# Norm factors spread over the partitions through a row in DRAM

## The chip, the cores and the metric

The kernel runs on one core of a Trainium2 chip. The metric is the time of one execution on the device in microseconds (us); a kernel's time is the median over its runs. Where the text names engines, PE is TensorE (PEld its weight loads), DVE is VectorE, ACT is ScalarE, POOL is GpSimd, and SP is SyncE, which here only issues DMAs. L700 means line 700 of the kernel before.

## The reference

One layer of a streaming encoder is computed for a prompt of 2048 tokens and a sample of 64 tokens, with 1024 features and 2816 hidden units in the MLP. All tensors are float32.

```
h  = rmsnorm(x, g1) * (1 + sc1) + sh1          # sc, sh, gt: six vectors made from the conditioning vector
u, q, k, v, o, gates = split(h @ w_in)
mix = concat(pool_mixer(u), mlstm(q, k, v, gates) normed per head, times sigmoid(o)) @ w_out
x  = x + gt1 * mix
h2 = rmsnorm(x, g2) * (1 + sc2) + sh2
a, g = split(causal depthwise conv of width 3 over (h2 @ w_up))
x  = x + gt2 * ((silu(g) * a) @ w_down)
y  = rmsnorm(x, g_final)
rmsnorm(x, g) = x * rsqrt(mean(x * x) + 1e-6) * g
```

Each of the three norms needs one factor per token, `rsqrt(mean(x * x) + 1e-6)`. It is this factor that the change is about.

## The kernel before

Activations lie transposed: features over the 128 partitions (8 tiles for 1024 features), tokens along the free axis. A factor per token has therefore to stand on all 128 partitions as the same row. The sums of squares over the partitions come out of matmuls (`rstd_rows`, `rstd_cols`, and in `final` a row of small matmuls), and POOL raises them to the power -0.5. They then stand as columns: token p of a chunk of 128 on partition p, one column to a chunk. Turning the columns into a row on all partitions is the work of two helpers.

`bcast` (attention stage) and `bcast_cols` (all later uses) do it in the same way. DVE multiplies the identity by the column, which gives diagonals. ACT rounds them to the matmul's float32r format, DVE takes the difference (the low half), and PE multiplies a matrix of ones by each half, so that every partition gets the sum over the diagonal, which is the row. ACT copies it from PSUM to a tile with the tag `rb`. Both are generators: each `yield` gives control back to the loop that feeds PE, and they are resumed by ticks between matmuls.

The work has two stages.

*Attention.* Four groups of 512 tokens, the last with the 64 sample tokens besides (576). For each group: the projections (`proj_v` at L1122, then per head `proj_qko`, then four projections for the pooling mixer in `U_ORDER`, all through `gemm` at L458), the mLSTM chunks, and the output projection `outproj`. Every product is three float32r matmuls (high times high, high times low, low times high), whose halves are made by ACT (L392) and DVE (L395) as the weights come in, some units ahead of PE. Side work stands in queues of generators: `bg[0]` to `bg[4]`, advanced by `tick(i)`, and `side`, advanced by `extra()`; `drain` runs a queue to its end. In queue 1 run `norm1` of the next group (squares, statistics, then `bcast`, whose result is in `box`), `norm_apply` of the next group (`modulate`, L559 to L562, which reads the row), and, during the last group, `norm_h` (L717), which applies the second norm to the first 704 tokens in 16 steps (8 tiles of features by two halves of 352 tokens) and stores the result in DRAM. The factors of the second norm are kept as columns in `RS2`, written at the end of each group by `rstd_rows` from `side`, or by `stat2` for the last group. In this stage a planner orders each engine's instructions; its estimates decide where a DMA stands in a queue.

*MLP.* Three groups of 704 tokens, `fgroups[0]` to `[2]`. Here the order on PE, ACT, DVE and POOL is that in which the program writes them; SP's is still the planner's. A `Pair` makes seven products (`product`, L1577, 12 matmuls of 352 columns each) in place of eight, from sums of operands that are made beforehand. ACT's copies from one PSUM bank to another (`seed`, L1624) stand between them. Each product ticks queue 0 twice and some places tick queue 1. The second half of the MLP follows in parts (L2143), or paired (`quad_down`, L2020). `prepare` (L791) runs in queue 1 and makes the operands of the next group: it spreads the factors of 704 tokens, loads the residual from DRAM (L801), norms it (L712, L715) and stores seven sums and their halves to DRAM (L813, issued from ACT). It runs for groups 1 and 2. `final` (L1878) runs in queue 0 during the next group's first part and applies the last norm to the group that has ended: statistics (L1884), `bcast_cols`, eight products on DVE (L1893) with four yields from one to the next, and a store for each (L1897). The residual's tiles are then loaded anew for the next group (L1865), once the store has read them, and the next sums into them are at L1992. The last group ends through another function, `final_end`.

Scratch tiles come from a ring of five in the attention stage (tag `scr`) and a ring of four in the MLP (tag `fscr`). Each `bcast` or `bcast_cols` takes three of them, for the diagonals and the two halves.

Of the kernel before, what the change touches and what calls it, by code (L numbers as in the profile page):

```python
# [9 lines left out]
F32 = mybir.dt.float32  # L10
F32R = mybir.dt.float32r
AF = mybir.ActivationFunctionType
ALU = mybir.AluOpType
# [51 lines left out]
def tile_layer(ctx: ExitStack, tc: tile.TileContext, xT, vecs, cst, rst, w_mod, w_ada, c_rows, w_qkou, w_v, w_pool,  # L65
# [21 lines left out]
    def m2_ps():  # L87
        return bank("m2")
# [11 lines left out]
    def scr():  # L100
        return sp.tile([P, TMAX], F32, tag="scr", name="scr")
# [427 lines left out]
    def bcast(rs, o, box):  # L529

        rb = sp.tile([P, TMAX], F32, tag="rb", name="rb", bufs=1)
        dg = scr()
        dh = sp.tile([P, TMAX], F32R, tag="scr", name="dh")
        dl = sp.tile([P, TMAX], F32R, tag="scr", name="dl")
        for (a, b, n, s) in o.tsegs:
            lo = a * P
            w = (b - a) * n
            v = dg[:n, lo:lo + w].rearrange("p (t c) -> p t c", c=n)
            dve.tensor_tensor(out=v, in0=ident[:n, :n].unsqueeze(1).broadcast_to([n, b - a, n]),
                              in1=rs[:n, a:b].unsqueeze(2).broadcast_to([n, b - a, n]), op=ALU.mult)  # L540
            act.activation(dh[:n, lo:lo + w], dg[:n, lo:lo + w], AF.Copy)
            dve.tensor_tensor(out=dl[:n, lo:lo + w], in0=dg[:n, lo:lo + w], in1=dh[:n, lo:lo + w].bitcast(F32),
                              op=ALU.subtract)
        yield
        yield
        for (a, b, n, s) in o.tsegs:
            lo = a * P
            w = (b - a) * n
            ps = m2_ps()
            pe.matmul(ps[:, :w], ones_r[:n, :], dh[:n, lo:lo + w], start=True, stop=False)  # L550
            pe.matmul(ps[:, :w], ones_r[:n, :], dl[:n, lo:lo + w], start=False, stop=True)
            act.activation(rb[:, lo:lo + w], ps[:, :w], AF.Copy)
        box.append(rb)
        yield

# [12 lines left out]
    RS2 = cp.tile([P, NCH], F32, tag="RS2", name="RS2")  # L568
    pool.memset(RS2, 0.0)
    RF = cp.tile([P, 6], F32, tag="RF", name="RF")  # L570
    pool.memset(RF, 0.0)

# [18 lines left out]
    def stat2(o, ssum):  # L591
        out = RS2[:, 4 * o.g:4 * o.g + len(o.chunks)]
        for _ in range(12):
            yield
        rstd_cols([ssum], o, out)
        yield

    def outproj(o, mix, between):
# [29 lines left out]
        if o.last:  # L628
            bg[0].append(stat2(o, ssum))
        else:  # L630
            side.append(rstd_rows(ssum, o, RS2[:, 4 * o.g:4 * o.g + len(o.chunks)], []))

# [40 lines left out]

    def bcast_cols(rs, t0, w, box, scr, r0=0):

        rb = scr("rb")
        dg, dh, dl = scr(), scr(F32R), scr(F32R)
        t = t0
        while t < t0 + w:
            c, a = divmod(t, P)  # L680
            n = 1
            if a == 0 and t + P <= t0 + w:
                n = (t0 + w - t) // P
                v = dg[:, t - t0:t - t0 + n * P].rearrange("p (t c) -> p t c", c=P)
                dve.tensor_tensor(out=v, in0=ident.unsqueeze(1).broadcast_to([P, n, P]),
                                  in1=rs[:, c:c + n].unsqueeze(2).broadcast_to([P, n, P]), op=ALU.mult)
                t += n * P
            else:
                e = min(P, a + t0 + w - t)
                dve.tensor_scalar(out=dg[:, t - t0:t - t0 + e - a], in0=ident[:, a:e], scalar1=rs[:, c:c + 1],  # L690
                                  scalar2=None, op0=ALU.mult)
                t += e - a
        yield
        act.activation(dh[:, :w], dg[:, :w], AF.Copy)
        dve.tensor_tensor(out=dl[:, :w], in0=dg[:, :w], in1=dh[:, :w].bitcast(F32), op=ALU.subtract)
        yield
        yield
        for lo in range(0, w, FH):
            ps = m2_ps()
            pe.matmul(ps[:, :FH], ones_r, dh[:, lo:lo + FH], start=True, stop=False)  # L700
            pe.matmul(ps[:, :FH], ones_r, dl[:, lo:lo + FH], start=False, stop=True)
            act.activation(rb[:, lo:lo + FH], ps[:, :FH], AF.Copy)
        box.append(rb)
        yield

    def normed(x, k, t0, w, rb, steps=(0, 1)):
# [10 lines left out]
    def norm_h(o, rows, scr):  # L717
# [11 lines left out]
        for h in range(2):  # L729
            yield from bcast_cols(RS2, o.t0 + h * FH, FH, box, lambda dt=F32: rows[10 + h] if dt == "rb" else scr(dt))  # L730
        for i, (t0, k) in enumerate(todo):
# [59 lines left out]
    def prepare(o, scr):  # L791

        box = []
        yield from bcast_cols(RS2, o.t0, FT, box, scr)
        yield
# [1082 lines left out]
    def final(o, x3, ssum):  # L1878
# [9 lines left out]
        box = []  # L1888
        yield from bcast_cols(RF, 0, FT, box, fscr)
        yield  # L1890
        yield
        for k in range(KD):
# [404 lines left out]
```

## Time and profile before

| | us |
|---|---|
| median of 3 runs | 2172.56 |
| lowest and highest run | 2170.78, 2175.88 |
| the profiled execution | 2170.94 |
| its span | 2169.1 |
| PE busy in the span | 2144.5 |
| DVE busy | 1629.4 |
| ACT busy | 1095.8 |
| POOL busy | 246.3 |

The span is what the profiler saw from the first to the last instruction; the execution's own time is 1.8 us longer. Busy times are not added up, since the engines work side by side. A row of a timeline gives start, duration, engine, line, operation, result and inputs, and how many instructions were merged, all in us from the start of the span. A row of a line's instructions gives the number, then the shortest, median and longest duration in ns, then the first and last start in us. A row of a stage gives its limits and width, then each engine's busy time with its number of instructions, then the granted PE clock (1 is full), the DMA engines' busy share and GB/s. A row of waits gives who waited for whom, the total in us, how often, and the longest. Rows of DMA issues end with the KB of each and the median time from issue to landing.

### The profile page before, as it was taken

How to read it: one execution, taken by the hardware profiler on the slowest of the kernel's cores; microseconds unless marked ns; L12 is line 12 of the kernel's file. 1: busy time of each engine (PE TensorE's matmuls, PEld its weight loads, DVE VectorE, ACT ScalarE, POOL GpSimd, SP SyncE). 2: the span in 40 equal slices, each digit the busy share in tenths (PEclk: the TensorE clock that was granted, in tenths of full speed). 3: DMA queues.
4: the chain of work that ended last, by engine and by line, in shares of the span. 5: the costliest groups of instructions: out<-in, count | busy, mean ns of one | idle time of the engine just before them, and what ended most of it. 6: DMA issues, size and time to landing. Idle time of an engine off the chain costs nothing.

```text
span 2169.1 us, 37944 instructions
## 1 busy us (share of the span) xinstructions
PE 2144.5 (99%) x13505; PEld 2041.6 (94%) x13505; DVE 1629.4 (75%) x3068; ACT 1095.8 (51%) x2182; POOL 246.3 (11%) x474
## 2 busy tenths in 40 slices
PE   8999999999999999999999999999999999999998
PEld 7788988888899999999999999999999999999998
DVE  5768769767964768797967668988886597887874
ACT  4455335334333446474636445655655365565554
POOL 0010001001000101010101220100100331111112
PEclk9999999999999999999999999999999999999999
DMA  8897988988886477888967976666668675555542
GB/s 313 305 325 254 348 327 278 344 324 289 279 310 221 155 250 236 290 291 303 346 216 247 322 257 210 233 218 203 224 222 278 221 255 182 175 176 187 175 160 78
DMA packets 245862, 543.63 MB, mean 251 GB/s; under 512 B 25252, under 2 KB 68772, under 8 KB 242856
## 3 DMA queue, kind: packets, MB, share of 16 engines
q1 hardware_dynamic: 236232, 518.89, 70.5%
q10 hardware_dynamic: 9440, 22.32, 2.6%
q8 instruction: 106, 1.74, 0.3%
q14 instruction: 84, 0.69, 0.1%
HBM read 415.12 MB, written 125.99 MB: 249 GB/s over the span
## 4 chain that ended last, share of the span: by engine, by line
PE 83%; DVE 5%; DMA 3%; issue 2%; ACT 1%; SPq 0%; POOL 0%; DVEq 0%; POOLq 0%; ACTq 0%
PE mm L1577 35%; PE mm L458 21%; PE mm L2143 12%; PE mm L2020 8%; PE mm L1122 3%; DVE wt L395 2%; PE m L1312 1%; PE m L1332 1%; PE m L1334 1%; PE m L1297 1%; DMA wt<-wsum 1%; DVE tg L1555 1%; DMA raw<-w_v 1%; DMA raw<-w_ada 0%; ACT tg L1550 0%
## 5 line engine op out<-in xcount | busy, mean ns | idle before, releaser
L1577 PE MATMUL mm<-hx,wt 128*128 128x352 f32 x5544 | 885.2, 321 | 0.8 <-DVE eg L1586 0.5
L1577 PEld LDWEIGHTS mm<-hx,wt 128*128 128x128 f32 x5544 | 878.9, 188 | 1.8 <-DVE wt L395 0.8
L458 PE MATMUL mm<-hl,wt 128*128 128x512 f32 (+2 forms) x1920 | 388.6, 357 | 0.0
L392 ACT ACTIVATE wt<-raw 128x512 fp32r<-128x512 f32 (+3 forms) x470 | 276.5, 597 | 180.6 <-PE mm L2143 49.7
L458 PEld LDWEIGHTS mm<-hl,wt 128*128 128x128 f32 x1920 | 316.3, 189 | 44.3 <-issue 1.1
L395 DVE TENSOR_TENSOR wt<-raw,wt 128x512 fp32r<-128x512 f32 (+3 forms) x470 | 312.7, 671 | 57.3 <-ACT wt L392 57.1
L2143 PE MATMUL mm<-av,wt 128*128 128x448 f32 (+1 forms) x1632 | 262.7, 322 | 0.0
L2143 PEld LDWEIGHTS mm<-av,wt 128*128 128x128 f32 x1632 | 250.4, 188 | 11.1
L1992 DVE SCALAR_TENSOR_TENSOR x<-mm,MOD,x 128x352 f32<-128x352 f32 (+3 forms) x360 | 167.5, 505 | 78.4 <-PE mm L2143 65.0
L2020 PE MATMUL mm<-av,wt 128*128 128x352 f32 x1344 | 220.8, 323 | 2.3 <-DVE x L1992 0.7
L2020 PEld LDWEIGHTS mm<-av,wt 128*128 128x128 f32 x1344 | 215.4, 188 | 5.4 <-DVE ea L1586 3.4
L1624 ACT ACTIVATE mm<-mm 128x352 f32<-128x352 f32 x196 | 87.8, 448 | 250.9 <-PE mm L1577 194.5
L458 PE MATMUL mm<-mx,wt 128*128 128x512 f32 (+1 forms) x960 | 183.1, 352 | 0.6 <-DVE scr L231 0.6
L458 PEld LDWEIGHTS mm<-mx,wt 128*128 128x128 f32 x960 | 159.4, 188 | 23.5 <-DVE scr L231 0.5
L1555 DVE SCALAR_TENSOR_TENSOR ta<-ea,V,ta 128x704 f32<-128x704 f32 (+1 forms) x132 | 125.7, 952 | 64.3 <-ACT ta L1550 51.9
L1555 DVE SCALAR_TENSOR_TENSOR tg<-eg,V,tg 128x704 f32<-128x704 f32 (+1 forms) x132 | 125.7, 953 | 59.9 <-ACT tg L1550 57.5
L395 DVE TENSOR_TENSOR wt<-wt 128x512 fp32r<-128x512 f32 x196 | 132.9, 684 | 12.8 <-ACT wt L392 12.7
L392 ACT ACTIVATE wt<-wt 128x512 fp32r<-128x512 f32 x196 | 120.1, 623 | 30.7 <-DMA wt<-wsum 25.4
L1764 ACT ACTIVATE tg<-tg 128x704 f32<-128x704 f32 (+1 forms) x66 | 52.4, 795 | 70.9 <-DVE tg L1555 70.9
L1533 POOL COPY ea<-UC 128x2 f32<-128x2 f32 x66 | 32.9, 498 | 483.4 <-DVE ta L1555 398.2
L1122 PE MATMUL mm<-wt,hl 128*128 128x256 f32 (+1 forms) x576 | 71.3, 284 | 0.0
L1122 PEld LDWEIGHTS mm<-wt,hl 128*128 128x128 f32 x576 | 70.4, 190 | 0.8 <-issue 0.6
(292 smaller groups left out, 2175.1 us busy)
## 6 DMA issues: line engine op xcount, KB each, us to landing
wt<-wsplit SPq DMA_DIRECT2D x132, 512.0 KB, 4.4
raw<-w_up SPq DMA_DIRECT2D x198, 256.0 KB, 4.1
wt<-hl_kept SPq DMA_DIRECT2D x96, 512.0 KB, 5.8
wt<-wsum SPq DMA_DIRECT2D x132, 256.0 KB, 5.0
wsplit<-wt SPq DMA_DIRECT2D x66, 512.0 KB, 5.8
w<-w_up SPq DMA_DIRECT2D x44, 512.0 KB, 5.8
wsum<-w SPq DMA_DIRECT2D x22, 1024.0 KB, 4.9
Bd<-fscr ACTq DMA_DIRECT2D x56, 352.0 KB, 4.3
```

What stands on the lines that cost most here:

```text
L392: act.activation(u.w[:, 0, :u.n], u.raw[:, :u.n], AF.Copy)
L395: dve.tensor_tensor(out=u.w[:, 1, :u.n], in0=u.raw[:, :u.n], in1=u.w[:, 0, :u.n].bitcast(F32), op=ALU.subtract)
L458: pe.matmul(ps[bi][:, :hi - lo], U[:, a, k % 4 * P:(k % 4 + 1) * P], mv[k][:, b, lo:hi], start=(at == 0 and pi == 0), stop=(k == order[-1] ...
L1122: pe.matmul(ps[ti][:n, :cols], h[4 * kh + k4][:, b, lo:lo + n], U[:, a, k4 % 2 * cols:(k4 % 2 + 1) * cols], start=(kh == 0 and k4 == 0 and ...
L1533: pool.tensor_copy(ext[:, 0:2], UC[:, f, :])
L1555: dve.scalar_tensor_tensor(out=t[:, :E], in0=ext[:, j:j + E], scalar=wc(j, f), in1=t[:, :E], op0=ALU.mult, op1=ALU.add)
L1577: pe.matmul(bk.t[:, :FH], U[:, a, kc * P:(kc + 1) * P], Bo.at(nm, kc, b), start=(first and kc == 0 and pi == 0), stop=(kc == 3 and pi == 2 ...
L1624: act.activation(to.t[:, :FH], bk.t[:, :FH], AF.Copy)
L1764: act.activation(self.tg[:, :E], self.tg[:, :E], AF.Silu)
L1992: dve.scalar_tensor_tensor(out=x3[n][:, a:b], in0=bk.t[:, a - lo:b - lo], scalar=gt2(n, s), in1=x3[n][:, a:b], op0=ALU.mult, op1=ALU.add)
L2020: pe.matmul(bk.t[:, :FH], U[:, a, c:c + P], quad.put(op, m, b), start=(first and m == 0 and pi == 0), stop=(m == 1 and pi == 2), skip_grou ...
L2143: pe.matmul(bks[i].t[:, :hi - lo], U[:, a, k % 4 * P:(k % 4 + 1) * P], av[k][:, b, lo:hi], start=(k == 0 and (a, b) == PASSES[0]), stop=(k ...
```

## The change

`bcast` and `bcast_cols` lose their diagonals, halves and matmuls. The columns are stored as a row of tokens in DRAM, and that row is loaded into the `rb` tile with a stride of zero over the partitions. All these DMAs are issued from ACT. `rows_out` stores and `spread_row` loads. For the second norm the row `r2d` is written when the statistics are made: `r2_out` stands behind `rstd_rows` in `side`, and `stat2` stores two yields after its statistics. `norm_h` then spreads both halves at once, followed by two yields in place of eight; `prepare` has two yields where it had five ahead of its first load. `final` stores the row four yields after its statistics in two DMAs (five whole chunks, and the rest of 64 tokens), spreads it five yields later, and its products begin five yields after that. The memsets of `RS2` and `RF` go. `final_end` and the first group's own norm stay as they were.

```diff
     def bcast(rs, o, box):
+        rd = dr.tile([TMAX], F32, tag=f"rn{o.g}", name=f"rn{o.g}")
+        rows_out(rd, rs, o)
+        yield
+        yield
         rb = sp.tile([P, TMAX], F32, tag="rb", name="rb", bufs=1)
-        dg = scr()
-        dh = sp.tile([P, TMAX], F32R, tag="scr", name="dh")
-        dl = sp.tile([P, TMAX], F32R, tag="scr", name="dl")
+        spread_row(rb, rd, 0, o.T)
+        box.append(rb)
+        yield
+
+    def rows_out(rd, rs, o):
         for (a, b, n, s) in o.tsegs:
             lo = a * P
...
+            act.dma_start(out=rd[lo:lo + (b - a) * n].rearrange("(c p) -> p c", p=n), in_=rs[:n, a:b])
+
+    def spread_row(out, rd, t0, w):
+        act.dma_start(out=out[:, :w], in_=rd[t0:t0 + w].unsqueeze(0).broadcast_to([P, w]))
...
     RS2 = cp.tile([P, NCH], F32, tag="RS2", name="RS2")
-    pool.memset(RS2, 0.0)
     RF = cp.tile([P, 6], F32, tag="RF", name="RF")
-    pool.memset(RF, 0.0)
+    r2d = dr.tile([NTOK], F32, tag="r2d", name="r2d")
...
         rstd_cols([ssum], o, out)
+        for _ in range(2):
+            yield
+        rows_out(r2d[o.t0:o.t0 + o.T], out, o)
+        yield
+
+    def r2_out(out, o):
+        rows_out(r2d[o.t0:o.t0 + o.T], out, o)
         yield
...
-            side.append(rstd_rows(ssum, o, RS2[:, 4 * o.g:4 * o.g + len(o.chunks)], []))
+            out = RS2[:, 4 * o.g:4 * o.g + len(o.chunks)]
+            side.append(rstd_rows(ssum, o, out, []))
+            side.append(r2_out(out, o))
...
-    def bcast_cols(rs, t0, w, box, scr, r0=0):
...
         for h in range(2):
-            yield from bcast_cols(RS2, o.t0 + h * FH, FH, box, lambda dt=F32: rows[10 + h] if dt == "rb" else scr(dt))
+            box.append(rows[10 + h])
+            spread_row(box[h], r2d, o.t0 + h * FH, FH)
+        yield
+        yield
...
     def prepare(o, scr):
         box = []
-        yield from bcast_cols(RS2, o.t0, FT, box, scr)
+        box.append(scr("rb"))
+        spread_row(box[0], r2d, o.t0, FT)
+        yield
         yield
...
         yield
         yield
         box = []
-        yield from bcast_cols(RF, 0, FT, box, fscr)
-        yield
-        yield
+        rd = dr.tile([6 * P], F32, tag=f"rf{o.g}", name=f"rf{o.g}")
+        for _ in range(2):
+            yield
+        nf, rest = divmod(FT, P)
+        act.dma_start(out=rd[:nf * P].rearrange("(c p) -> p c", p=P), in_=RF[:, :nf])
+        act.dma_start(out=rd[nf * P:FT].unsqueeze(1), in_=RF[:rest, nf:nf + 1])
+        for _ in range(5):
+            yield
+        box.append(fscr("rb"))
+        spread_row(box[0], rd, 0, FT)
+        for _ in range(5):
+            yield
```

More of the change, by code (lines that the diff above doesn't have):

```diff
@@ L529, in bcast @@
     def bcast(rs, o, box):
+        rd = dr.tile([TMAX], F32, tag=f"rn{o.g}", name=f"rn{o.g}")
+        rows_out(rd, rs, o)
+        yield
+        yield
         rb = sp.tile([P, TMAX], F32, tag="rb", name="rb", bufs=1)
-        dg = scr()
-        dh = sp.tile([P, TMAX], F32R, tag="scr", name="dh")
-        dl = sp.tile([P, TMAX], F32R, tag="scr", name="dl")
+        spread_row(rb, rd, 0, o.T)
+        box.append(rb)
+        yield
+    def rows_out(rd, rs, o):
         for (a, b, n, s) in o.tsegs:
             lo = a * P
[L537 to L543, printed above, removed]
-        yield
-        yield
[L546 to L554, printed above, removed]
+            act.dma_start(out=rd[lo:lo + (b - a) * n].rearrange("(c p) -> p c", p=n), in_=rs[:n, a:b])
+    def spread_row(out, rd, t0, w):
+        act.dma_start(out=out[:, :w], in_=rd[t0:t0 + w].unsqueeze(0).broadcast_to([P, w]))
     def modulate(dst, x, k, rb, G, sh, o):
@@ L672, in at @@
             return self.tiles[nm, kc // 2][:, kc % 2, part, HO:HO + FH]
-    def bcast_cols(rs, t0, w, box, scr, r0=0):
[L676 to L704, printed above, removed]
     def normed(x, k, t0, w, rb, steps=(0, 1)):
@@ L1888, in final @@
         box = []
-        yield from bcast_cols(RF, 0, FT, box, fscr)
-        yield
-        yield
+        rd = dr.tile([6 * P], F32, tag=f"rf{o.g}", name=f"rf{o.g}")
[10 more added lines that the diff above has]
+            yield
         for k in range(KD):
```

## The prediction

> **What bounds the kernel now.** I read the page's busy times and its chain first, then a table of stages, then the removed instructions one by one, and last the DMAs whose like the change adds.
>
> ```profile
> PE 2144.5 (99%) x13505; PEld 2041.6 (94%) x13505; DVE 1629.4 (75%) x3068; ACT 1095.8 (51%) x2182; POOL 246.3 (11%) x474
> ...
> PE 83%; DVE 5%; DMA 3%; issue 2%; ACT 1%; SPq 0%; POOL 0%; DVEq 0%; POOLq 0%; ACTq 0%
> ```
>
> PE is busy for 2144.5 of 2169.1 us, and 83% of the chain that ended last is PE's. The table of stages (width, then busy time of PE, PEld, DVE, ACT and POOL) shows where the rest lies.
>
> ```profile
> 200.00:788.00 588.00, 586.51 (x3646) 527.38 (x3645) 426.39 (x927) 233.82 (x575) 42.82 (x58) 1.00 0.81 283
> ...
> 867.00:1160.00 293.00, 292.26 (x1840) 286.81 (x1839) 233.00 (x406) 158.88 (x291) 22.10 (x50) 1.00 0.84 285
> ...
> 1313.00:1707.00 394.00, 392.11 (x2456) 387.92 (x2455) 316.65 (x516) 225.37 (x414) 40.02 (x78) 1.00 0.68 224
> ```
>
> In the attention stage after the start (200 to 788) PE idles 1.5 us of 588; in the two stretches in which `prepare` runs (867 to 1160, 1313 to 1707) it idles 0.7 and 1.9 us. So a matmul that goes is worth the time that it holds PE. DVE and ACT have slack, and what they lose is worth nothing by itself; the danger is that something new makes PE wait.
>
> **What goes: 28 matmuls.** By the program, `bcast` runs three times (two matmuls of 512 columns each, and once two of 64 columns), `norm_h` calls `bcast_cols` twice with one block of 352 columns, `prepare` and `final` twice each with two blocks. With two matmuls to a block that makes 8 on L550 and L551 and 20 on L700 and L701. The row is the busy time of the ten on L700 over the whole span; L701 has as many.
>
> ```profile
> 0.00:2169.00 2169.00, 3.21 (x10) 1.88 (x10) 1.00 0.74 251
> ```
>
> That is 0.32 us each, but these durations overlap: the next matmul starts after half of it. What it holds of PE is read from start to start, in the timeline of PE.
>
> ```profile
> 173.73 0.39 PE L550 MATMUL m<-dh,ones_r 128*128 128x512 f32 x1
> ...
> 174.19 1.09 PE L458 MATMUL mm<-mx,wt 128*128 128x512 f32 x4
> ...
> 527.98 0.39 PE L550 MATMUL m<-dh,ones_r 128*128 128x512 f32 x1
> ...
> 528.87 1.42 PE L458 MATMUL mm<-mx,wt 128*128 128x512 f32 x5
> ...
> 871.17 0.32 PE L700 MATMUL m<-fscr,ones_r 128*128 128x352 f32 x1
> ...
> 871.81 1.53 PE L2143 MATMUL mm<-av,wt 128*128 128x256 f32 x8
> ```
>
> A pair of 512 columns holds PE 174.19 - 173.73 = 0.46 us, and there are two groups with just that; the group with the sample tokens holds it 528.87 - 527.98 = 0.89. Four matmuls of 352 columns hold it 871.81 - 871.17 = 0.64, or 0.16 each. The sum: 2 x 0.46 + 0.89 + 20 x 0.16 = 5.0 us. No row shows PE idle ahead of one of them, so all of it should come back.
>
> The Trainium skill's "TensorE: Matmul & The Clock Gate", section "Back-to-back issue gap", gives an isolated gap of columns / 2.4 + 2.5 ns. By it the 28 would be worth an estimated 4.3 us. This trace has 0.16 us where the formula has 0.149 and 0.23 where it has 0.216, so the measured 5.0 stands.
>
> The 27 DVE instructions (diagonals, low halves) and 24 ACT instructions (high halves, copies out of PSUM) that go too are counted at nothing: PE covers them now. The two memsets of `RS2` and `RF` lie at the start on POOL, which is 11% busy: nothing.
>
> **What comes: 22 DMAs on ACT's queue.** 13 write a row (4 in `bcast`, 5 for `RS2`, 4 in `final`), word by word, since neighbouring tokens lie on neighbouring partitions; 9 spread it (3, 2 in `norm_h`, 2 in `prepare`, 2 in `final`). Nearest rows:
>
> ```profile
> L813 ACTq DMA_DIRECT2D Bd<-fscr x56: 326/326/348, 884.0 to 1631.0; - x56
> ...
> DMA to landing us min/median/max: 2.2/4.3/6.7
> ```
>
> ```profile
> fscr<-x2d SPq DMA_DIRECT2D x16, 352.0 KB, 5.6
> ...
> s<-cs SPq DMA_DIRECT2D x8, 256.0 KB, 4.7
> ...
> scr<-cst SPq DMA_DIRECT2D x1, 2.0 KB, 3.6
> ```
>
> ```profile
> L667 SPq DMA_DIRECT2D hx<-Bd x56: 523/562/1277, 1197.8 to 1685.0; - x56
> ```
>
> To issue one takes ACT 0.33 us (`Bd`), at most what the longest of `hx` took, 1.28: 22 make 7 to 28 us of ACT's sequencer. ACT is busy half of the time, and the ACT work that goes makes room; I count nothing. A spread is a load from one DRAM row with stride zero, like `s<-cs`: 4.7 us to landing, and 2.2 to 6.7 by the other rows. A row write has no like; the nearest are the 2 KB that `scr<-cst` moved in 128 pieces of 16 bytes (3.6 us) and the stores of `Bd`. I take 2.2 to 6.7 for it as well, and 4 as the value, since the row nearest in size says 3.6. Both ends go into the range.
>
> **Who waits, site by site.** In `bcast` the spread stands behind the row write on ACT, two steps later.
>
> ```profile
> L559 DVE SCALAR_TENSOR_TENSOR scr<-hl,G,rb x32: 277/744/752, 178.1 to 561.4; 128x512 f32<-128x512 f32 x24, 128x64 f32<-128x64 f32 x8
> ```
>
> ```profile
> 217.91 14.56 PE mm L1122 x120
> ```
>
> A step is a projection of 24 matmuls of 512 columns at 0.23 us, so two steps are 11 us, over the 6.7 that a write may take. The spread goes out where the matmuls stand now, by 174, and lands by 181; the first reader stands at 178.1. That is up to 3 us of DVE, and the group that needs the result starts its projections (L1122) at 217.9. Nothing.
>
> The rows of `RS2` are written two attention groups or more ahead of their readers, so `norm_h` and `prepare` wait for the spread alone. `norm_h` starts its 16 steps six yields earlier, in a stretch where PE had no idle time: nothing.
>
> `prepare` reaches its first product three yields earlier. In the first of its two runs:
>
> ```profile
> 867.10 0.25 DVE L690 TENSOR_SCALAR fscr<-V,RS 128x64 f32<-128x64 f32 x1
> ...
> 869.13 1.58 SPq L801 DMA_DIRECT2D fscr<-x2d  x2
> ...
> 877.74 0.95 DVE L712 SCALAR_TENSOR_TENSOR fscr<-fscr,G,rb 128x704 f32<-128x704 f32 x1
> ```
>
> Seven yields took 10.6 us, or 1.5 each, so the product moves to four yields after the spread, about 873.2. The spread is there by 874 at the latest; the rows loaded at 869.1 to 870.7 would land at 876.3 by the 5.6 us above, unless the freed `fscr` buffers let them go earlier. That is 0 to 3 us of DVE with weight splits queued behind it, against which stand units split ahead. I take nothing, and up to 1 us for the range. Beyond that, all of `prepare`'s later work meets other pieces of the products than now. The idle time in its stretches, 0.7 + 1.9 = 2.6 us, is what such meetings cost now: the shift can win it or cost as much again. I take zero between those.
>
> `final` is the one place where ACT can stand.
>
> ```profile
> L1893 DVE SCALAR_TENSOR_TENSOR x<-x,V,rb x8: 941/946/948, 1267.1 to 1295.0; 128x704 f32<-128x704 f32 x8
> ```
>
> ```profile
> ACT mm L1624 <- PE mm L1577: 194.5, 115, 5.2
> ```
>
> Eight products with four yields between them spread over 27.9 us: 1.0 us a yield. The row goes out four yields after the statistics, the spread follows five later, the first product five after that, 14 where there were 8. If the write lands 4 us after its issue, ACT doesn't wait; at 6.7 and two issues it waits about 2.4. Behind the wait are the copies that seed PE's banks (L1624). ACT waits for PE ahead of them 194.5 / 115 = 1.7 us now, so at most 0.7 us reaches PE, 1.4 for the two runs. I take nothing. DVE may wait up to 2 us for the spread; its next work is weight splits, with units in hand.
>
> The product of the last row moves from 1295.0 to about 1301, and with it the store and the load that reuses its buffer on SP.
>
> ```profile
> L1865 SPq DMA_DIRECT2D x<-x2d x8: 319/351/462, 1272.3 to 1300.3; - x8
> ```
>
> ```profile
> 1326.16 1.07 DVE L1992 SCALAR_TENSOR_TENSOR x<-mm,MOD,x 128x352 f32<-128x352 f32 x2
> ```
>
> The last load goes out at about 1306 and lands by 1313; the first sum into these rows is at 1326.2. Hidden, with 13 us to spare. SP waits for the stores as now, at other moments.
>
> **Sum.** -5.0 on PE, zero taken for the rest, bounds -2.6 and +2.6 (shift), +1.4 (`final`), +1.0 (`prepare`). The profiled execution took 2170.94 us, 1.6 below the median of 2172.56 (runs from 2170.78 to 2175.88); set against the median the result is 2167.6.
>
> **Rivals.** (1) *Given back.* PE gets its 5.0, and the new meetings in `prepare` and the waits take them again: 2172.56 - 5.0 + 2.6 + 1.4 + 1.0 = 2172.6 at the most, which is no change. For it: DVE is 80% busy in those stretches, and the idle time there is real. Against it: less work is left there than before.
>
> (2) *Late rows; this one ends slower.* If a row of 640 single words takes as long as five of the 128-piece loads, it lands after 5 x 3.6 = 18 us. ACT then stands in `final` for 18 - 5 = 13 us; 1.7 us of its own idle time and one product of 12 matmuls (1.9 us) cover 3.6, and 9.4 us reach PE, twice: 2172.56 - 5.0 + 18.8 = 2186.4. It decides once a write lands later than 5.0 + 3.6 + 2.5 = 11.1 us; below that the sum is still a gain. Against it: 3.6 us for 128 pieces is no more than what 256 KB take, so the number of pieces hardly shows. The Trainium skill speaks for it: "DMA: Bandwidth & Descriptors", section "Rules for kernel authors", says that a last dimension that isn't contiguous is lowered to one descriptor for each element, and to rearrange it. No run here shows a write of that kind in numbers that decide it.
>
> (3) *More than the matmuls.* The shift of `prepare` clears its 2.6 us as well: 2172.56 - 7.6 = 2165.0. For it: two DVE and two ACT passes over 704 columns leave the second `prepare` just where a paired product begins.
>
> (4) *It does nothing*, since PE would only wait longer at the next point. Against it: with 1.5 us idle in 588 there is no such point in the attention stage; in `prepare` it is part of (1).
>
> **How the numbers follow.** A measurement of this kernel can tell about 0.2%, or 4.3 us, from no change; the forecast lies 0.7 us beyond that. The forecast has a chance of 0.45 (its own range 2165 to 2169), (3) 0.08, (1) with all that ends between -4.3 and +4.3 us 0.30, (2) and milder forms of it 0.17; (4) is held in (1). So faster 0.53, the same 0.30, slower 0.17. The range runs from a microsecond below (3), 2164, to the upper end of (1) with the spread of the runs shown above it, about 2175.
>
> **What would show it.** Right: 28 matmuls fewer on PE; PE's idle time from 200 to 2150 still about 5 us; the row writes landing within 7 us; the first product of `final` 6 us later; no wait of ACT above 3 us for a row. Wrong: ACT standing at the spread in `final` and PE idle behind it; more idle time in the two stretches of `prepare`; a weight load behind a blocked SP.

## The result, and the profile after

The changed kernel takes 2251.59 us (median of 4 runs, 2248.20 to 2253.51), the kernel before 2171.67 us in the same comparison (4 runs, 2170.73 to 2175.88). The ratio is 1.0363, with a 95% interval from 1.0351 to 1.0375: 80 us slower, where 5 us faster was forecast. Line numbers from here on are those of the kernel that the fence is from; in the changed one `rows_out` is L544, `spread_row` L548, `final`'s row writes L1868 and L1869, the paired product L1552 (L1577 before).

Two lines of the page of the changed kernel: the busy times, and the shares of the chain that ended last.

```profile
PE 2162.5 (96%) x13477; PEld 2054.4 (91%) x13477; DVE 1617.0 (72%) x3041; ACT 1084.4 (48%) x2158; POOL 241.6 (11%) x472
...
PE 71%; DMA 6%; DVE 5%; issue 2%; ACT 2%; POOL 0%; ACTq 0%; SPq 0%; DVEq 0%; POOLq 0%
```

The 28 matmuls are gone (13505 to 13477), yet PE is busy for 18 us more and idle for 2251.8 - 2162.5 = 89.3 us where it was 24.6. PE's share of the chain fell from 83% to 71%, and DMA's rose from 3% to 6%. The extra busy time goes with a lower granted clock: 0.983 in the mean (0.998 before), and 0.96 in the first of the three stages below. The table is cut at about the same pieces of work as the one of before.

```profile
213.00:844.00 631.00, 596.63 (x3638) 535.07 (x3637) 423.04 (x917) 231.33 (x567) 42.41 (x58) 0.96 0.82 265
929.00:1222.00 293.00, 291.89 (x1836) 285.81 (x1835) 231.04 (x402) 157.02 (x288) 21.60 (x50) 1.00 0.84 285
1381.00:1782.00 401.00, 395.79 (x2453) 391.08 (x2452) 315.35 (x513) 223.61 (x412) 39.51 (x78) 1.00 0.67 222
```

The attention stretch is 43 us wider (631 for 588), and PE idles 34.4 us in it where it idled 1.5. The first stretch of `prepare` is unchanged, in the second PE idles 5.2 us for 1.9. The first paired product shows the same:

```profile
L1552 PE MATMUL mm<-hx,wt x5544: 317/322/661, 844.5 to 2196.8; 128*128 128x352 f32 x198
```

It starts at 844.5 us, in the kernel before at 788.5. So 56 us, of the 82.6 between the two profiled executions, are lost by the end of the attention stage.

What the new DMAs take, by the list of DMA issues (KB of each, median us from issue to landing):

```profile
rb<-rf ACTq DMA_DIRECT2D x2, 352.0 KB, 5.1
rb<-rn ACTq DMA_DIRECT2D x2, 256.0 KB, 5.0
...
rn<-rs ACTq DMA_DIRECT2D x3, 2.0 KB, 14.7
rf<-RF ACTq DMA_DIRECT2D x2, 2.5 KB, 10.7
rf<-RF ACTq DMA_DIRECT2D x2, 0.2 KB, 12.0
```

The spreads land as forecast, after 5 us. The row writes take 11 to 15 us, about three times the 4 us of the forecast, for 2 KB. The engines' waits show who stood for them:

```profile
ACT mm L1599 <- DMA rf<-RF: 24.1, 2, 13.0
...
PE m L1307 <- DVE st L231: 24.9, 3, 9.7
...
PE mm L1341 <- DVE nd L231: 14.2, 2, 13.5
PE mm L1552 <- ACT mm L1599: 13.7, 4, 5.8
...
ACT nd L231 <- DMA rn<-rs: 12.7, 1, 12.7
ACT mx L484 <- DMA rn<-rs: 12.5, 1, 12.5
ACT scr L231 <- DMA rn<-rs: 11.3, 1, 11.3
```

In the kernel before, the rows of PE's like waits are these; it has none behind `st` or behind ACT's copies between PSUM banks:

```profile
PE m L1312 <- DVE kw L231: 3.8, 2, 3.0
PE mm L1366 <- DVE nd L231: 2.1, 2, 1.4
...
PE mm L2020 <- DVE ea L1586: 0.6, 1, 0.6
```

ACT stands 60.6 us in five places, three of them in `bcast`, which the forecast had held for safe. The timeline of the first shows the path to PE:

```profile
152.98 0.40 ACTq L544 DMA_DIRECT2D rn<-rs  x1
...
155.78 0.28 ACT L231 ACTIVATE nd<-m 128x129 f32<-128x129 f32 x1 [0.25 <-PE m L1307]
...
168.40 0.36 ACTq L548 DMA_DIRECT2D rb<-rn  x1
168.81 0.62 ACT L231 ACTIVATE nd<-m 128x129 f32<-128x129 f32 x3 [12.75 <-DMA rn<-rs]
...
174.88 1.12 PE L1341 MATMUL mm<-V,nd 128*128 128x128 f32 x4 [13.46 <-DVE nd L231]
```

ACT sends the row off at 152.98, does a few copies up to 156, and then stands at the spread, which may only go out when the row has landed, at 168.40. Behind it in ACT's order stand the mLSTM's copies (`nd`), behind these DVE's product, behind that PE's, which waits 13.46 us.

Such a wait costs more than its length. In the window from the spread on, the clock granted to PE is 0.57 in the mean:

```profile
168.40:180.00 11.60, 5.12 (x18) 4.27 (x19) 9.32 (x21) 5.92 (x19) 1.72 (x3) 0.57 0.80 268
```

The trace has eight stretches at half clock before the end of the products, each at a wait of PE, and together 72 us long; the kernel before has one of 3.4 us. The matmuls in them take longer: the longest of the paired products took 661 ns, for a median of 322 (row L1552 above). Counting the end of the span too, which is at half clock in both kernels, PE is busy at half clock for 36.0 us, and in the kernel before for 5.0; half of the difference, 15.5 us, is an estimate of what the clock adds to PE's busy time.

The second kind of loss has no engine waiting for a row. The rows of the second norm have their first reader at 630.9 us, by the view of the instructions on `r2d`:

```profile
L548 ACTq DMA_DIRECT2D mx<-r2d x2: 338/349/360, 630.9 to 632.2; - x2
```

and this is what the first of their writes does 360 us earlier:

```profile
271.54 0.37 ACTq L544 DMA_DIRECT2D r2d<-RS  x1
...
274.01 0.70 SPq L195 DMA_DIRECT2D raw<-w_ada  x1
274.76 12.14 SPq L376 DMA_DIRECT2D wt<-hl_kept  x2
...
287.52 0.75 DVE L208 CUSTOM_DVE_ANT_0 junk<-raw,s,MOD 128x512 f32<-128x512 f32 x1 [6.83 <-DMA raw<-w_ada]
...
289.37 0.31 ACT L231 ACTIVATE jk<-nd 128x128 f32<-128x128 f32 x1 [6.83 <-DVE nd L231]
```

A load of weights that SP issued 2.5 us after the write is waited for by DVE until 287.5; it landed after 13.5 us, and the same load of the kernel before, at 259.5 us, after 7.5. DVE stands 6.8 us for it, and ACT as long behind DVE. SP's next two issues take 12.1 us, since SP stands between them. The waits of SP's queue, from 270 to 300 us, say for what:

```profile
SPq L376 <- DMA r2d<-RS: 11.3, 1, 11.3
```

SP waits until the row write has landed, though it doesn't read the row. By the trace the DMAs of SP and ACT use the same eight semaphores in turn, and SP's issue takes up the one that the row write had taken, so it stands until that write is done. In the whole kernel SP stands 57.2 us in this way, and issues no loads meanwhile. The DMA engines are not idle meanwhile. The table of windows says so for this place and for the first row of `final` (the last three numbers are the granted clock, the DMA engines' busy share, and GB/s):

```profile
276.00:290.00 14.00, 13.89 (x75) 11.63 (x74) 6.65 (x17) 1.57 (x8) 0.00 (x0) 1.00 0.91 180
1325.20:1337.80 12.60, 9.44 (x60) 9.15 (x58) 1.65 (x3) 1.07 (x2) 0.31 (x3) 1.00 0.92 94
```

They are busy for 91 and 92% of the time and move 180 and 94 GB/s; in the stage table of before they moved 283 GB/s at a share of 0.81 and 224 at 0.68. So there were two theories to tell apart: *waiting* (engines stand because their next instruction needs the row) and *holding* (a slow row write makes other DMAs late, and the weights with them). Holding has two parts that look alike in the time: loads in flight beside the write take longer, and SP's next loads are issued late, since SP stands for the write. A third, rival 1 of the prediction, is the *shift* of the steps behind the spreads.

### The profile page after: what moved, and what is told of

It reads as the page before. It is cut to its first block, busy times and chain, and to the rows that moved or that the text cites. A ratio compares the mean times of both kernels' runs of the same rounds, so it can differ in the third digit from the quotient of the medians.

```text
span 2251.8 us, 37879 instructions
## 1 busy us (share of the span) xinstructions
PE 2162.5 (96%) x13477; PEld 2054.4 (91%) x13477; DVE 1617.0 (72%) x3041; ACT 1084.4 (48%) x2158; POOL 241.6 (11%) x472
## 4 chain that ended last, share of the span: by engine, by line
PE 71%; DMA 6%; DVE 5%; issue 2%; ACT 2%; POOL 0%; ACTq 0%; SPq 0%; DVEq 0%; POOLq 0%
PE mm L1552 34%; PE mm L458 13%; PE mm L2127 11%; PE mm L2004 8%; DMA rf<-RF 1%; DVE wt L395 1%; PE mm L1097 1%; DMA raw<-w_ada 1%; DMA wsum<-w 1%; DMA rn<-rs 1%; PE m L1307 1%; DMA wt<-wsum 1%; DMA wsplit<-wt 1%; PE m L1309 1%; PE m L1287 0%
## 5 line engine op out<-in xcount | busy, mean ns | idle before, releaser
L1552 PE MATMUL mm<-hx,wt 128*128 128x352 f32 x5544 | 895.6, 323 | 15.4 <-ACT mm L1599 13.7
L1552 PEld LDWEIGHTS mm<-hx,wt 128*128 128x128 f32 x5544 | 886.9, 189 | 18.9 <-ACT mm L1599 14.8
L458 PE MATMUL mm<-hl,wt 128*128 128x512 f32 (+2 forms) x1920 | 394.5, 361 | 0.1
L2127 PEld LDWEIGHTS mm<-av,wt 128*128 128x128 f32 x1632 | 250.4, 188 | 11.5 <-DVE wt L395 0.4
```

Source lines behind the costliest of these rows:

```text
L458: pe.matmul(ps[bi][:, :hi - lo], U[:, a, k % 4 * P:(k % 4 + 1) * P], mv[k][:, b, lo:hi], start=(at == 0 and pi == 0), stop=(k == order[-1] ...
L1552: pe.matmul(bk.t[:, :FH], U[:, a, kc * P:(kc + 1) * P], Bo.at(nm, kc, b), start=(first and kc == 0 and pi == 0), stop=(kc == 3 and pi == 2 ...
L2127: pe.matmul(bks[i].t[:, :hi - lo], U[:, a, k % 4 * P:(k % 4 + 1) * P], av[k][:, b, lo:hi], start=(k == 0 and (a, b) == PASSES[0]), stop=(k ...
```

## The experiments

All ratios are against the kernel before, measured beside each, whose medians lay between 2171.0 and 2172.7 us.

**1. The row writes alone** (`w_words`). The kernel before, diagonals and all, plus the 13 writes at the places where the change has them.

```diff
     def bcast(rs, o, box):
+        rows_out(dr.tile([TMAX], F32, ...), 0, rs, o)
...
+            act.dma_start(out=rd[lo:lo + (b - a) * n].rearrange("(c p) -> p c", p=n), in_=rs[:n, a:b])
```

> The kernel before, with its diagonals and matmuls, and besides all 13 row writes of the change, word by word, into DRAM that nobody reads. No engine waits for them as data. Standing theory (the 80 us come from ACT waiting behind its own row write, at the three bcast and the two final): 2172 to 2176, since no wait is left. Holding theory (a row write keeps the DMA engines from finishing anything else for 11 to 15 us, so that weight loads come late whoever waits for the row): 2195 to 2225, about the 20 us that the four writes of RS2 seem to have cost, and as much again for the other writes; single-word writes land after 11 to 15 us in both.

Measured: 2224.76 us, ratio 1.0240 (1.0221 to 1.0260), 53 us slower. The instructions on the row `r2d`, PE's waits, and two of the waits of SP's queue, in that kernel:

```profile
L534 ACTq DMA_DIRECT2D r2d<-RS x5: 366/373/464, 267.4 to 838.9; - x5
...
DMA to landing us min/median/max: 10.3/13.3/15.9
```

```profile
PE mm L1601 <- ACT mm L1648: 10.0, 5, 2.9
PE mm L1390 <- DVE nd L231: 8.9, 2, 8.1
PE m L1336 <- DVE kw L231: 8.7, 3, 5.2
PE m L1356 <- DVE st L231: 6.8, 1, 6.8
```

```profile
SPq L371 <- DMA rn<-rs: 30.3, 3, 12.0
...
SPq L376 <- DMA r2d<-RS: 21.9, 2, 11.5
```

No engine that computes waits for a row, and PE still waits for DVE and ACT in the places where it does in the changed kernel. So two thirds of the loss is holding. But SP's queue stands for the unread rows too, 61.8 us in all, and so this run doesn't tell the two parts of holding apart. In one place it does: at the second `final` write (1764.8 us) SP stands for no row, yet a load (`wt<-wsum`) that SP issued 0.5 us behind the write is what ACT waits 6.2 us for, until 1777.8, and PE stands 2.9 us behind ACT. Loads of this kind land after 5.0 us in the median; this one took about 12.5. There a slower load reached PE without SP's standing.

**2. The same words in other shapes** (`w_pieces`, `w_apart`, `w_apart64`, `w_apart16`, `w_apart8`). Again only unread writes are added. In the first, a partition's four words lie beside each other, so that a write is 128 pieces of 16 bytes (the rests of 64 tokens stay single words). In the others the 512 words stay single, but lie 512, 64, 16 or 8 bytes from one to the next.

```diff
-    out=rd[lo:lo + (b - a) * n].rearrange("(c p) -> p c", p=n)
+    out=rd[lo:lo + (b - a) * n].rearrange("(p c) -> p c", p=n)              # w_pieces
+    out=rd[...].rearrange("(c p w) -> p c w", p=n, w=128)[:, :, 0:1]         # w_apart; w = 16, 4, 2 in the others
```

> As the one with all row writes beside the matmuls, but each partition's four or five words are stored side by side, so that a write of 512 words is 128 pieces of 16 bytes over the same 2 KB (the order in DRAM is then not that of the tokens; nobody reads it). If the time goes with the number of pieces: landing 3 to 5 us, time at most 2177. If it goes with the bytes or the region written: landing 11 to 15 us and the same time as with single words.

> The kernel before with the 13 row writes added and nobody reading them, as in the run with the words, but each word goes to an address 512 bytes from the last one, so that no two words lie near each other in DRAM. Theory A, it is the number of single words that makes a write late and holds the other DMAs: landings stay at 11 to 15 us, and the time at 2215 to 2235 us. Theory B, it is that words beside each other are written one into the other's stretch of memory: landings fall to 2 to 6 us, and the time to 2172 to 2185 us.

> The kernel before with the 13 unread row writes, single words 64 bytes from each other. Words with no gap cost 53 us, words 512 bytes apart nothing that can be measured (2173.7 us). Theory A, what matters is how many single words fall into one short stretch of 64 bytes: here it is one, the landings stay at 5 to 7 us and the time at 2171 to 2176 us. Theory B, the stretch that counts is 512 bytes long: here eight words fall into one, landings go to 8 to 11 us, the time to 2185 to 2210 us.

> The same with 16 bytes from word to word, so that four words fall into 64 bytes and 32 into 512 bytes; their number is still 512. Theory A (64 bytes): as many writes into each stretch as in the run with pieces of 16 bytes, so 2180 to 2190 us, landings 6 to 9 us. Theory B (512 bytes): nearly as bad as the words without a gap, 2205 to 2225 us, landings 10 to 13 us. Theory C, only whether words touch each other counts (a write that the next one is joined to): 2171 to 2176 us.

> The kernel before with the 13 unread row writes, single words 8 bytes from each other: no two touch, two fall into each stretch of 16 bytes. Touching theory: no loss, 2171 to 2176 us, landings 5 to 7 us as with gaps of 16 bytes and more. Stretch theory: two writes meet in each 16 bytes, where it was one, and four without gaps: a part of the 53 us, 2182 to 2205 us, landings 8 to 11 us.

| the word's neighbour | time, us | ratio (95%) |
|---|---|---|
| touches it, 512 words (`w_words`) | 2224.76 | 1.0240 (1.0221 to 1.0260) |
| 8 bytes on (`w_apart8`) | 2183.98 | 1.0056 (1.0040 to 1.0073) |
| 16 bytes on (`w_apart16`) | 2173.08 | 1.0007 (0.9998 to 1.0017) |
| 64 bytes on (`w_apart64`) | 2172.51 | 1.0003 (0.9994 to 1.0012) |
| 512 bytes on (`w_apart`) | 2173.74 | 1.0008 (0.9999 to 1.0017) |
| touches it, in 128 pieces of 16 bytes (`w_pieces`) | 2182.29 | 1.0048 (1.0033 to 1.0063) |

The landings of the `r2d` writes (the trace has them for four of the five, one of these the rest of 64 tokens), for 8, 16 and 512 bytes in this order:

```profile
DMA to landing us min/median/max: 6.0/9.1/11.6
```

```profile
DMA to landing us min/median/max: 5.3/6.7/10.0
```

```profile
DMA to landing us min/median/max: 4.0/5.8/9.5
```

Neither expectation of `w_pieces` (at most 2177 us, or the time of the single words) was met; its `r2d` writes landed after 5.3 to 9.3 us.

The number of packets doesn't explain the table. ACT's queue has this row on the page of the kernel with touching words and on that with 16 bytes from word to word:

```profile
q10 hardware_dynamic: 14768, 22.34, 2.8%
```

The two are alike to the packet and 52 us apart. What differs is what the DMA engines achieve. These windows of 12 us begin about 1.5 us after the first `r2d` write, with words that touch and with 512 bytes between them:

```profile
269.00:281.00 12.00, 12.00 (x72) 10.48 (x72) 4.83 (x9) 2.47 (x8) 0.00 (x0) 1.00 1.03 198
```

```profile
262.00:274.00 12.00, 12.00 (x73) 10.47 (x72) 8.10 (x20) 4.16 (x17) 0.00 (x0) 1.00 0.89 330
```

With touching words 198 GB/s pass at a full share, with words apart 330 at 0.89. DVE has 4.83 us of work in the one and 8.10 in the other, which goes with weights that come late; PE is still fed here and stands later. A part of the lower rate is SP, which stands 11.5 us for the touching words and 6.2 for the others. The rest shows in the packets of the loads: of SP's queue, those of 4 KB that start in these windows took 295 ns in the mean beside touching words, and 170 beside words apart. Over the whole kernel, the loads of weights that SP issued within 4 us of a row write (the 47 to 49 whose landing the trace has) landed after 11.6 us in the median with touching words, 8.0 with 8 bytes from word to word, 6.2 with 16 and 5.6 with 512; SP stood for row writes 61.8, 31.5, 23.5 and 18.1 us. So beside touching words the loads in flight are slower, and SP stands longer; which part of the 53 us is which, no run shows. Eight bytes apart, where two words share 16 bytes, a part of the loss is there (12 us); from 16 bytes on it is gone. That goes with a cost for several writes into the same 16 bytes and against the idea that only touching counts. The pieces of 16 bytes cost 10 us though no two share 16 bytes; four of their thirteen writes are rests of 64 touching words, which landed after 9 to 10 us, but whether these four make the 10 us was not tried.

The Trainium skill's "DMA: Bandwidth & Descriptors", section "Specifications", says that transfers below 512 bytes are done by read-modify-write. No run here shows whether that is what takes the time; the size alone doesn't decide it, since words of 4 bytes that lie 16 bytes or more apart cost the kernel nothing that can be measured. The same page of the Trainium skill, section "Rules for kernel authors", says that issuing from SP, ACT and GpSimd doesn't add bandwidth, since all use the same 16 engines. The traces agree: beside a write from ACT's queue, loads in flight on SP's landed after 11.6 us in the median with touching words, for 5.6 with words 512 bytes apart.

**3. Half of the change** (`r2_only`, `rest_only`). The first has the change for the second norm alone, with `bcast` and `final` as before; the second is its complement.

> The change done for the second norm alone (RS2 written as a row, norm_h and prepare spread it); bcast and final as before. Nobody stands on ACT for these writes, since the readers come a group later. Standing theory: 2168 to 2171 (12 matmuls of 352 columns fewer, 1.9 us, and no loss). Holding theory: 2185 to 2200, four writes with 4 to 7 us of PE each, as read off the changed kernel at 271, 666 and 860 us.

> The change for the first and the last norm alone; the second norm goes by diagonals as before. Its complement, the second norm alone, cost 28.3 us. If the parts add up, this one costs 80 - 28 = 52 us, that is 2223 us (2218 to 2229). If they share what they cost (one late queue for both), it is more than 52 us, above 2232 us; if the one makes the other worse, less, below 2212 us.

Measured: 2199.96 us, 1.0128 (1.0113 to 1.0143), and 2218.25 us, 1.0213 (1.0193 to 1.0232). These are 28.3 and 47.2 us, together 75.5 of the 79.9: nearly additive. The half in which, of all engines, SP alone stands for a write (22.6 us by its queue's waits) still costs 28 us. PE's waits in `r2_only`:

```profile
PE m L1336 <- DVE kw L231: 9.0, 3, 5.4
...
PE mm L2044 <- DVE ea L1610: 5.2, 3, 1.9
```

The first is the holding, as in experiment 1 (3.8 us in the kernel before). The second, at the MLP's second half, is not in the kernel before (0.6 us there), and comes back in experiments 4 and 5.

**4. Rows for nothing** (`const_rows`, `const_words`, `const_keep`). The spreads read a row of the input, so that no spread has a write to wait for, and the norms' factors are left out. Then the 13 writes are put back, unread. Then, without writes, the steps behind the second norm's spreads are set back to where they were before the change.

```diff
-        spread_row(rb, rd, 0, o.T)
+        spread_row(rb, xT[0, 0], 0, o.T)
...
-        yield                       # const_keep: 8 yields in norm_h and 5 in prepare, for 2 and 2
-        yield
+        for _ in range(8):
+            yield
```

> The change with its row writes left out; its spreads read a row of the input in place of the factors (so the norms are left out, and the steps and the spreads are those of the change). Nobody waits for a row here. Waiting theory: with the writes and the waits gone, what is left is 28 matmuls of 5.0 us fewer, so 2166 to 2171 us. Shift theory: the consumers of the second norm's factors, which come 3 to 6 turns of the planner earlier, cost what they cost with the turned rows (6 to 9 us): 2174 to 2181 us.

> The same with the 13 row writes word by word put back, read by nobody. Holding theory: the time of the run without the writes plus the 53 us that these writes cost the kernel before, and the changed kernel's rest (2251.6 minus this) is the wait for the row: 2219 to 2234 us. If the waits for the row are hidden behind the same hold-up, it is within 5 us of the changed kernel, 2246 to 2256 us.

> The change with its row writes left out and its spreads reading a row of the input (the norms are left out), and with the steps behind the second norm's spreads as many planner's turns behind as before (8 and 5 for 2 and 2). Shift theory: the 6.5 us that the same without the turns cost go, and with 28 matmuls fewer it is 2165 to 2170 us, which is the most that any form of this change can give. Rival, the cost lies in the spreads' own transfers (nine, of 176 to 352 KB): it stays at 2174 to 2180 us, and then no form of the change gains.

Measured: without writes 2178.37 us, 1.0034 (1.0023 to 1.0044); with writes 2228.99 us, 1.0265 (1.0242 to 1.0289); without writes and with the old distances 2173.51 us, 1.0002 (0.9992 to 1.0012). So the 80 us divide into three: 6.5 us that the change costs even with rows for nothing, 50.6 us that the unread writes add by holding, and 2251.6 - 2229.0 = 22.6 us that come once the rows are read, which is the engines' waiting. The border between the last two is good to about 5 us, by the interval of `const_words`; and with no row to wait for the spreads go out earlier, the first of `bcast` at 42.2 us for 168.4. The 6.5 us are the shift: set back, they are gone, and with them one wait of PE. First `const_rows`, then `const_keep`:

```profile
PE mm L1996 <- DVE ea L1556: 4.7, 3, 1.9
```

```profile
PE mm L1996 <- DVE ea L1556: 0.9, 1, 0.9
```

The last result says more, and it misses the 2165 to 2170 us that were expected. There 28 matmuls are gone, no row is written, no spread has a write to wait for, and the time is the same as before: the 5.0 us of the matmuls don't show either (the interval ends at 0.08% or 1.7 us below). This kernel still has the nine spreads and the later steps of `final`, so whether the 5.0 us are not won, or won and spent there, no run tells. Its busy line shows PE 3.5 us less busy than before, and PE's idle time in the span is 26.8 us for 24.6:

```profile
PE 2141.0 (99%) x13477; PEld 2038.7 (94%) x13477; DVE 1615.4 (75%) x3041; ACT 1085.8 (50%) x2158; POOL 244.8 (11%) x472
```

**5. Rows that land early** (`turned`, `turned_wait`, `turned_keep`, `turned_late`). The factors are the real ones here. PE turns the columns into rows by a small transpose, DVE copies them out of PSUM, and the row goes to DRAM in pieces of 512 bytes. The later three are steps on from it: four more yields ahead of the second norm's transposes; then also the old distances of 8 and 5; then also `bcast` by diagonals again.

```diff
+            pe.transpose(pt[:b - a, ...], rs[:n, a:b], ident[:n, :n])
...
+            dve.tensor_copy(row[:b - a, c:c + n], pt[:b - a, c:c + n])
...
+            act.dma_start(out=rd[a * P:a * P + (b - a) * n].rearrange("(c p) -> c p", p=n), in_=row[:b - a, c:c + n])
```

> The change with one step put in: PE turns the columns into rows first (a transpose of 128 by 4 or 5), DVE copies them out of PSUM, and the row goes to DRAM in 4 or 5 pieces of 512 bytes. All waits behind the row write stay where the change has them. Both theories: the write lands in 2 to 5 us, ACT stands 0 to 3 us at each of five places, PE has 28 matmuls less and 13 transposes of about 0.1 us more: 2166 to 2173. If it is the store and load through DRAM itself that costs, whatever the pieces: 2230 to 2255.

> The rows turned by a transpose and written in pieces of 512 bytes, with four more turns of the planner between the second norm's pow and its transposes. In the run without them TensorE stood 5.3 us for that pow. If that wait is a loss of its own, the time falls by 4 to 6 us from 2199 us, to 2193 to 2195 us; if the work behind is late for another reason (the shift of the second norm's other steps), it stays within 2 us of 2199 us.

> As the run with the transposes set further back, and besides the steps behind the spreads of the second norm's factors stand as many planner's turns behind as they stood in the kernel before (8 and 5, where the change has 2 and 2). If what is left of the loss without the slow writes is the shift of these steps, the time falls to 2165 to 2175 us: 28 matmuls of 5.0 us are gone and 13 small transposes of about 3 us with their loads have come. If it comes from the spreads' transfers of 352 and 256 KB or from the vector engine's added copies, it stays at 2190 to 2196 us.

> The second and the last norm by rows that a transpose has turned, with the steps behind the spreads as late as before; the first norm's spread by diagonals as before. With the first norm by rows too it was 2184.4 us, 13 us over the kernel before. If what is left of the loss is the first norm's round trip through DRAM, which the next product waits for, the time is 2168 to 2173 us: 20 of the 28 matmuls (3.2 us) are gone, 9 small transposes with their loads (about 2 us) have come. If the loss is the second norm's, it stays at 2179 to 2185 us.

Measured: 2199.05 us, 1.0127 (1.0110 to 1.0144); 2190.46 us, 1.0087 (1.0071 to 1.0104); 2184.40 us, 1.0055 (1.0037 to 1.0073); 2179.93 us, 1.0039 (1.0026 to 1.0052). With the rows turned the writes are no longer late; the timeline of the first `bcast`:

```profile
169.04 0.52 ACTq L557 DMA_DIRECT2D rn<-scr  x1
171.42 0.37 ACTq L564 DMA_DIRECT2D rb<-rn  x1
```

The spread goes out 2.4 us after the write, for 15.4 in the changed kernel, and 53 of the 80 us are back. That this is as many as the unread writes cost in experiment 1 is chance: here the long waits for a row end too, and transposes come. The expectation of 2166 to 2173 us was missed by 26. PE's waits in `turned` name two of the steps that remain:

```profile
PE m L543 <- POOL RS L526: 5.3, 3, 3.5
PE mm L2019 <- DVE ea L1577: 5.2, 4, 1.9
```

The first is of this version's own making: the transposes stood right behind POOL's power, and four yields more gave 8 us (27.4 over the kernel before, then 19.5), more than the wait itself. The second is the shift again; the old distances gave another 6 us. But the expectation of 2165 to 2175 us for `turned_keep` was missed, and so was 2168 to 2173 for `turned_late`, by 7 us. Of those 8 us (1.0039), PE's idle time has 4.3 in the profiled execution (28.9 us for 24.6) and its busy time 4.4 (2148.9 for 2144.5, with 11 matmuls fewer); what causes them stays open. No form that was run is faster than the kernel before, and the one with rows for nothing only equals it.

## Why the prediction was wrong

**The landing of a row write** is the step that failed. The prediction took 4 us from the row "nearest in size", `scr<-cst`, and 2.2 to 6.7 us as bounds. Measured were 10.7 to 14.7 (the three that the changed kernel's trace has). That row was a load in pieces of 16 bytes; the new thing about the write was its single words at neighbouring addresses in DRAM, and no row of the trace before bounded that. Rival 2 had the lateness (18 us, deciding from 11.1) with a chance of 0.17. It was set back by the argument that "the number of pieces hardly shows". That argument was right in itself (512 words set 16 bytes apart or more cost nothing), but the number of pieces was not what mattered. The same number of packets with touching words costs 53 us.

**Who pays for a late write** failed as well, also in rival 2. It counted ACT's wait in `final` alone, 13 us twice, of which 18.8 reach PE. That was near: ACT stands there 24.1 us in two waits, and PE behind its copies 13.7. But ACT stands longer in `bcast` (36.5 us in three). The sentence on `bcast` assumed that the spread goes out two steps, or 11 us, later "where the matmuls stand now". In the trace the order of ACT has it 3 us of copies behind the write, and ACT stands there from 156 to 168.4. What reading the rows adds to the time, all waiting together, is 22.6 us (experiment 4).

**What was left out** is the largest term: 50.6 us (53 in the kernel before) for the other DMAs that a row write makes late. The prediction said of the second norm's rows that `norm_h` and `prepare` "wait for the spread alone". That is true, and still the second norm's half costs 28.3 us, of which the shift is about 6 by experiment 4. It also said that "SP waits for the stores as now, at other moments"; SP stands 57.2 us for row writes that it doesn't read. The prediction asked who reads the row, and neither what else the 16 DMA engines had to move at that moment, although the stage table of before shows them busy for 0.81 of the attention stretch, nor which queue's next issue stands behind the write. How the 50.6 us divide between slower loads and SP's standing stays open.

**The shift** was bounded by 2.6 us either way and taken as zero; it costs 5.7 us (const_rows against const_keep, 6.5 and 0.8 over the kernel before). The step that failed is the bound: the idle time that `prepare`'s stretches have now was taken for the most that new meetings can cost. The wait that the shift made lies in the second of these stretches, in the paired second half of the MLP (`quad_down`, L1996 in `const_rows`, at 1406.7, 1489.9 and 1572.2 us), and with rows for nothing PE idles 5.4 us from 1313 to 1707, where it idled 1.9.

**The matmuls** were 28, as counted, and the changed kernel has 28 fewer. "All of it should come back" has no run for it: `const_keep` excludes a gain above 1.7 us. Its outcome is that of rivals 1 and 4, no change, but it doesn't say which of them holds. By the profiled executions PE is 3.5 us less busy there and idles 2.2 us more; no run takes out the matmuls alone, without the spreads, so where the gain goes is not settled.

**What was right**: the spreads (5 us, taken 4.7), their count and places, that DVE's and ACT's removed work is worth nothing by itself (`const_keep` gains nothing), and the list of signs, of which "ACT standing at the spread in `final` and PE idle behind it" and "a weight load behind a blocked SP" both came.

## What to carry to other kernels

Cost a new DMA by the pattern of its addresses in DRAM too, and not by its bytes or the nearest load: single words that fill a row from many partitions, each touching the next, landed late here, and made the loads beside them late, read or not. Where the DMA engines are busy for most of a stage, ask of each new DMA what it delays, before asking who reads it, and look at the waits of the queue that issues the loads: it can stand for a write that nobody reads. If a row has to go out, turn it first, so that its pieces are long; words set 16 bytes apart cost nothing unread, but a row read back from them was not tried. Test with unread writes, which separate the cost of a transfer from the cost of waiting for its data. And count a wait of PE with the slower clock behind it.

## What the runs showed of the hardware

A write of 512 single words of 4 bytes (`r2d`) landed after 10.3 to 15.9 us when the words touch in DRAM (9.0 to 15.0 in `r2_only`), after 6.0 to 11.6 with 8 bytes from word to word, and after 5.3 to 10.0 with 16. As four pieces of 512 bytes the first row was there within 2.4 us, when the spread behind it went out. While the first kind ran, the DMA engines moved 198 GB/s at a full share, where they moved 330 beside words set apart; a part of that is SP, which stood for the write. After PE had stood 13.5 us, the granted clock was 0.57 over the next stretch of 11.6 us. The gap of 16 bytes at which the loss ends was not expected, and the cause behind it was not measured.
